# Pairs of heads in one two-bank PSUM tile, and the output projection begun with attention and retention instead of pooling and convolution

## The chip, the cores and the metric

The kernel runs on one core of a Trainium2 chip. The metric is device time in microseconds (us) for one launch. Lower is better. The engines are called as the profile calls them: PE is TensorE (PEld its weight loads), DVE is VectorE, ACT is ScalarE, POOL is GpSimd, SP is SyncE, whose queue issues nearly all DMAs here.

## The reference, cut to what matters

Two layers of a decoder trunk, 512 tokens, model width 1024, all in float32. In each layer four mixers of 256 channels read one input projection, and one output projection reads the four of them side by side:

```python
h = rmsnorm(x, norm_mix_g[l]) * (1.0 + sc1) + sh1
u = h @ w_in[l]
fq, fk, fv, ff, pu, rq, rk, rv, rg, cu = jnp.split(u, bounds, axis=-1)
y_fox  = fox_attention(fq, fk, fv, ff, fox_fb[l])       # 4 heads x 64, forgetting attention
y_pool = pool_mixer(pu, pool_w[l], pool_scale[l])       # causal means over 2/4/8/16 tokens
y_ret  = retention(rq, rk, rv, rg, positions, ret_gn_g[l])   # 4 heads x 64, chunks of 128
y_conv = conformer_conv(cu, conv_w[l], ...)             # GLU, depthwise 31 taps, LayerNorm, swish
mix = jnp.concatenate([y_fox, y_pool, y_ret, y_conv], axis=-1)
x = x + g1 * (mix @ w_out[l])
h = rmsnorm(x, norm_ffn_g[l]) * (1.0 + sc2) + sh2
x = x + g2 * ((jax.nn.silu(h @ ffn_w1[l]) * (h @ ffn_w3[l])) @ ffn_w2[l])
```

The shifts, scales and gates (sh, sc, g) are products of the vector c with a 1024 x 6144 matrix in each layer, and a last RMSNorm follows.

## The kernel before

**Layout.** Activations are held transposed: 128 channels on the partitions, 512 tokens along the free axis, eight such chunks. Each large operand is split into a high part that fits the fast fp32r format and a low rest (`yh`, `yl` for the normed input, `ah`, `al` for mixer outputs, `wh`, `wl` for weights), and each product is three matmuls, `mm3`, lines 265 to 267: high x high, low x high, high x low. Weights come through the SP queue into `raw`, ACT casts `wh` (line 164), DVE subtracts `wl` (line 169); `plan` lists them in the order of their use, `take` and `rel` walk along it. The small products of attention and retention are plain float32 matmuls, and each leaves two records in the trace.

**PSUM.** Eight banks: a ring "mm" of three for projection results (`bank`), a ring "sm" of four for everything else (`small`), and one bank `aux` for sums of a few columns.

**Order of the work.** The text emits the projections in the order of the list `MO` (`pu` pooling input, `rk`, `rq`, `rv`, `rg` retention's key, query, value and gate, `o` two columns of the first half of the output projection). Beside them run generators: `conv_gen` (31 taps as DVE steps of two per yield, line 740, then a LayerNorm, lines 744 to 763), `fox_gen` (attention), `ret_gen` (one for each pair of retention's heads), `pool_mix`, and `ada_gen` (modulation sums on DVE, line 320, from `ada` tiles that DMA brings). Each call of `slot()` after a projection or half of one advances every generator by its rate (`r_conv`, `r_fox` and so on for layer 0, `q_...` for layer 1); `finish_bg` runs one to its end. `FB` steps of attention are emitted as soon as it starts. This text order is what the program states as priority: the last lines of the kernel pass `schedule_with_timeline_sim=True`, so a planner may issue ready work of lower priority earlier on an engine, and each engine then runs its list in order.

**Attention.** For each pair of heads and each block i of 128 queries: `scores` multiplies (line 812, one matmul for each head on 64 rows of the array, into a `small` each), reduces and normalises on DVE and ACT (lines 818 to 829); `turn` transposes the probabilities (line 838) and copies them to "PT" (line 840); `weigh` multiplies with the values (line 850, 64 columns for each head) into one bank held over the four blocks, which `split` turns into a pair of `ah` and `al` after the last. The steps of neighbouring blocks overlap.

**Output projection.** Columns of 128 outputs read eight mixer chunks: 0 and 1 attention, 2 and 3 pooling, 4 and 5 retention, 6 and 7 convolution. The first pass (`do_o`) takes pooling and convolution, chunks 2, 3, 6, 7, for all eight columns and adds them to the residual (line 1052); its first call finishes pooling and convolution. The second pass takes chunks 0, 1, 4, 5 with `N1` columns' banks open at first, finishing attention before chunk 0 and retention before chunk 4. Then follow the second norm and the feed-forward part in three segments; `adaV` generators (rate `r_adaV`, `q_adaV`) sum the remaining modulations beside it, and the end of the first segment finishes whatever runs.

Of the kernel before, what the change touches and what calls it, by code (L numbers as in the profile page):

```python
# [33 lines left out]
KN = {'GA': 3, 'GA1': 3, 'TR': 'V', 'NH': 5, 'NH1': 5, 'ST': ((0, 1), (1, 1), (2, 2), (4, 1), (5, 1), (6, 1), (7, 1)), 'MO': 'pu rk rq rg rv o o o o', 'MO1': 'pu rk rv rq o o o rg o', 'GK': 4, 'RD': 'sync', 'MM': 3, 'SM': 4, 'FB': 1, 'FB1': 2, 'OUTP': 0.0, 'FRONT': 1, 'FRONT1': 0, 'r_rot': 2, 'r_ada': 0.6, 'r_conv': 0.7, 'r_fox': 0.85, 'r_ret': 1, 'r_pool': 0.3, 'r_adaV': 0.4, 'q_conv': 1, 'q_fox': 1.2, 'q_ret': 2, 'q_pool': 0.4, 'q_adaV': 1, 'bP': 4, 'bPT': 2, 'bt': 3, 'brx': 2, 'bmx': 6, 'br8': 4, 'bpl': 3, 'brP': 3, 'bada': 3, 'bacs': 3, 'NR': 2, 'NW': 4, 'N1': 3, 'N11': 1, 'YLG': 9, 'SC': ('AVPPPGPA', 'GGPAVVPP', 'VVVVVVPP', 'VVVVVGVP', 'AAVPAVVP', 'VVVVVVVP', 'VVVVVVVP', 'AAVPAVVP'), 'SH': ('AVAPPPPP', 'VPPPPPAP', 'AAGAAAPP', 'AAAAAAPP', 'AAAAAAGP', 'AVVGAAVG', 'AAAAAAPP', 'AAAAAAPP'), 'MS': '', 'OF': {'lc': -1.907, 'lwq': -2.817, 'lw': -2.364, 'lh': -2.036, 'sc': -1.65, 'ds': 0.034, 'sh': -2.846, 'pc': -0.763, 'mc': -2.466, 'ph': -0.991, 'mh': 0.907, 't': 0.871, 'yh': -1.858, 'yl': 0.927, 'wh': -0.208, 'wl': -2.386, 'whq': -1.469, 'wlq': -0.219, 'mm': 0.333, 'mq': -0.566, 'dq': 0.84}, 'KB': (-4.084, -0.552, 1.672, 3.163, 4.202, 4.915, 6.134, 7.492), 'OA': (1, 0, 2, 3), 'OA1': (0, 1, 3, 2), 'OB': (1, 2, 0, 3), 'OB1': (1, 3, 0, 2), 'OUTP1': 3.0}  # L34
# [3 lines left out]
BUFS = dict(pw=2, ada=KN["bada"], ared=2, qk=4, acs=KN["bacs"], v=2, ff1=1, ff2=1, ff3=1, ff4=1, cumD=2, P=KN["bP"], rP=KN["brP"], PT=KN["bPT"], mx=KN["bmx"], cb=1,  # L38
# [7 lines left out]
def trunk(ctx, tc, x, c, positions, ada_w, ada_b, norm_mix_g, norm_ffn_g, w_in, fox_fb,  # L46
# [26 lines left out]
    def bank():  # L73
        return ps.tile([P, S], F32, tag="mm", name=nm("mm"), bufs=KN["MM"])
# [4 lines left out]
    def banks_of(n):  # L79
        return [bank() if i < KN["MM"] else small() for i in range(n)]  # L80
# [105 lines left out]
    for l in range(DEPTH):  # L186
        lstart.append(len(plan))
        if l == 0:
            for kh in range(2):
                plan += [wcol(w_in, 0, COL["cu"], 512, kh * 4 + k, 1) for k in range(4)]  # L190
                plan.append(wcol(w_in, 0, COL["fq"], 256, kh * 4, 4))
        else:
            plan += [wcol(w_in, l, n0) for n0 in CU]
            plan += [wcol(w_in, l, j * P) for j in range(2)]
        plan += [wcol(w_in, l, COL["fk"] + j * P) for j in range(2)]
        plan += [wcol(w_in, l, COL["fv"], 260, 4 * kh, 4) for kh in range(2)]
        outs = 0
# [8 lines left out]
        plan += [wout(l, i, 0) for i in range(4)]  # L206
# [25 lines left out]
    cur = dict(layer=0, on=0.0)  # L232
# [548 lines left out]
    def fox_gen(l, q, k, v):  # L781
# [17 lines left out]
        cds, prob, prT, outp = {}, {}, {}, {}  # L799
# [6 lines left out]
        def scores(pair, i):  # L806

            w = (i + 1) * P
            sts = [small(), small()]
            for hh in range(2):  # L810
                r0 = 64 * hh
                PE.matmul(sts[hh][:, 0:w], q[pair][r0:r0 + 64, i * P:w], k[pair][r0:r0 + 64, 0:w], start=True, stop=True)  # L812
            for hh in range(2):
                h, st = 2 * pair + hh, sts[hh]
# [17 lines left out]
        def turn(pair, i):  # L832
            w = (i + 1) * P
            for h in (2 * pair, 2 * pair + 1):
                pr = prob.pop((h, i))
# [3 lines left out]
                prT[h, i] = tmp("PT")  # L839
                A.copy(prT[h, i][:, 0:w], tt[:, 0:w])  # L840

        def weigh(pair, i):

            if i == 0:
                outp[pair] = small()
            pts = [prT.pop((2 * pair + hh, i)) for hh in range(2)]
            for j in range(i + 1):
                for hh in range(2):
                    h = 2 * pair + hh
                    PE.matmul(outp[pair][64 * hh:64 * hh + 64, i * P:(i + 1) * P], v[:, j, h * 64:(h + 1) * 64],  # L850
                              pts[hh][:, j * P:(j + 1) * P], start=j == 0, stop=j == i)
            if i == 3:
                mix[pair] = act_pair(pair)
                split(mix[pair], outp[pair])
# [34 lines left out]
    def ret_gen(l, pair, q, k, vbox, outs, sg):  # L889
# [11 lines left out]
        sts = [small(), small()]  # L901
        for n in range(4):
            for hh in range(2):
                r0 = 64 * hh
                PE.matmul(sts[hh][:, n * P:(n + 1) * P], k[r0:r0 + 64, n * P:(n + 1) * P],
                          q[r0:r0 + 64, n * P:(n + 1) * P], start=True, stop=True)
        prs = []
        for hh in range(2):
            h = 2 * pair + hh
            pr = tmp("rP")  # L910
            V.tensor_tensor(out=tri(pr, P), in0=tri(sts[hh], P),
                            in1=tri(cs[:, C_DM + h * P:C_DM + (h + 1) * P], P).to_broadcast([P, 4, P]), op=ALU.mult)
            prs.append(pr)
# [22 lines left out]
        for n in range(4):  # L936
            for hh in range(2):
                h = 2 * pair + hh
                PE.matmul(po[64 * hh:64 * hh + 64, n * P:(n + 1) * P], v[:, n, h * 64:(h + 1) * 64],
                          prs[hh][:, n * P:(n + 1) * P], start=n == 0, stop=False)  # L940
# [122 lines left out]
    for l in range(DEPTH):  # L1063
        cur["layer"] = l
        cur["on"] = 0.0
        early = []
# [79 lines left out]
        def do_o():  # L1146
            if not outs:
                finish_bg(pg)
                finish_bg([cg])
# [71 lines left out]

        start_bg("adaV", ada_gen(l, (5,)))
# [105 lines left out]
```

## Time and profile before

| | |
|---|---|
| median of 3 runs | 1254.05 us (1253.93 to 1257.28) |
| the profiled execution | 1255.27 us, of which the span is 1253.5 us |
| PE busy | 1209.0 us, 96% |
| DVE busy | 761.2 us, 61% |
| ACT busy | 406.5 us, 32% |
| mean granted PE clock | 0.974 |

The page cuts the span into 40 equal slices and gives the busy share of each engine in tenths; PEclk is the clock that PE was granted, in tenths of full speed. The views of the trace list instructions as line, engine, operation, and output <- inputs by the program's tile names; x2 after a row is a count, and brackets hold idle time before the row and what ended it. Lines are those of the kernel before.

### The profile page before, as it was taken

What the parts mean: (1) busy time and instruction counts of PE and PEld (TensorE: products, weight loads), DVE (VectorE), ACT (ScalarE), POOL (GpSimd) and SP (SyncE); (2) the same over time, 40 slices, a digit from 0 to 9 for tenths busy, and PEclk for the clock granted to TensorE, in tenths of its full rate; (3) what the DMA queues carried; (4) which work ended last, traced back from release to release, by engine and by line L of the source; (5) the groups of instructions that cost most, each with busy time, mean ns of one, the idle gap of its engine ahead of it and who ended that gap; (6) DMA issues with size and microseconds to landing.
All of it is one profiled execution on the core that took longest, in us unless ns stands there. A gap on an engine that the chain in (4) does not pass through costs nothing.

```text
span 1253.5 us, 16762 instructions
## 1 busy us (share of the span) xinstructions
PE 1209.0 (96%) x6373; PEld 1004.1 (80%) x6373; DVE 761.2 (61%) x1332; ACT 406.5 (32%) x654; POOL 95.5 (8%) x186
## 2 busy tenths in 40 slices
PE   9999989999998999999999999899999999999997
PEld 8778666789876888888899886678988888888887
DVE  6799997577777555453357998457653333333333
ACT  5433334244322222123234244424432223213222
POOL 5432210102000000000000000000100000000000
PEclk8999978999998999999999999899999999999999
DMA  9766622226777545343233343022443323233321
GB/s 308 215 207 187 201 86 76 68 68 190 244 226 239 167 135 173 103 137 97 75 96 95 96 130 84 9 94 84 154 149 101 99 86 99 74 113 101 95 74 68
DMA packets 223721, 160.05 MB, mean 128 GB/s; under 512 B 8374, under 2 KB 198032, under 8 KB 223640
## 3 DMA queue, kind: packets, MB, share of 16 engines
q1 hardware_dynamic: 223464, 158.90, 42.7%
q8 instruction: 50, 0.82, 0.3%
q14 instruction: 31, 0.25, 0.1%
q10 hardware_dynamic: 176, 0.08, 0.0%
HBM read 154.74 MB, written 2.11 MB: 125 GB/s over the span
## 4 chain that ended last, share of the span: by engine, by line
PE 74%; DMA 5%; DVE 4%; issue 1%; ACT 1%; POOL 0%; DVEq 0%; ACTq 0%
PE mm L265 22%; PE mm L266 22%; PE mm L267 22%; DMA ada<-in_ada_w 4%; DVE acs L320 1%; PE sm L812 1%; PE sm L850 1%; PE sm L265 1%; PE sm L266 1%; PE sm L267 1%; DVE wl L169 1%; DMA raw<-in_ffn_w 1%; PE sm L838 1%; PE aux L404 0%; PE sm L961 0%
## 5 line engine op out<-in xcount | busy, mean ns | idle before, releaser
L164 ACT CAST wh<-raw 128x1024 fp32r<-128x1024 f32 (+3 forms) x196 | 198.8, 1015 | 592.4 <-PE mm L266 385.0
L266 PE MATMUL mm<-yl,wh 128*128 128x512 f32 (+1 forms) x984 | 373.1, 381 | 2.2 <-DVE yl L442 2.1
L265 PE MATMUL mm<-yh,wh 128*128 128x512 f32 (+1 forms) x984 | 369.5, 382 | 5.2 <-ACT yh L438 5.2
L267 PE MATMUL mm<-yh,wl 128*128 128x512 f32 (+1 forms) x984 | 372.1, 379 | 0.0
L169 DVE TENSOR_TENSOR wl<-raw,wh 128x1024 fp32r<-128x1024 f32 (+3 forms) x196 | 231.7, 1183 | 137.8 <-ACT wh L164 131.2
L266 PEld LDWEIGHTS mm<-yl,wh 128*128 128x128 f32 x984 | 188.1, 191 | 38.6 <-DVE yl L442 3.5
L265 PEld LDWEIGHTS mm<-yh,wh 128*128 128x128 f32 x984 | 185.4, 191 | 40.6 <-ACT yh L438 6.2
L267 PEld LDWEIGHTS mm<-yh,wl 128*128 128x128 f32 x984 | 188.0, 191 | 36.3 <-issue 0.2
L265 PE MATMUL mm<-ah,wh 128*128 128x512 f32 (+1 forms) x516 | 189.4, 370 | 6.2 <-ACT ah L479 6.2
L266 PE MATMUL mm<-al,wh 128*128 128x512 f32 (+1 forms) x516 | 189.8, 368 | 0.8 <-DVE al L480 0.8
L267 PE MATMUL mm<-ah,wl 128*128 128x512 f32 (+1 forms) x516 | 188.7, 367 | 0.0
L320 DVE SCALAR_TENSOR_TENSOR acs<-ada,cact,acs 128x512 f32<-128x512 f32 x140 | 104.8, 748 | 42.6 <-DMA ada<-in_ada_w 40.4
L1052 DVE SCALAR_TENSOR_TENSOR xT<-mm,mod,xT 128x512 f32<-128x512 f32 (+1 forms) x86 | 57.7, 675 | 117.1 <-PE mm L267 116.8
L265 PEld LDWEIGHTS mm<-ah,wh 128*128 128x128 f32 x516 | 97.3, 189 | 24.0 <-ACT ah L479 6.8
L266 PEld LDWEIGHTS mm<-al,wh 128*128 128x128 f32 x516 | 97.6, 189 | 17.7 <-DVE al L480 1.2
L267 PEld LDWEIGHTS mm<-ah,wl 128*128 128x128 f32 x516 | 97.6, 189 | 17.1 <-issue 0.2
L1232 DVE TENSOR_TENSOR t<-t,mm 128x512 f32<-128x512 f32 x42 | 28.8, 685 | 100.5 <-PE mm L267 100.5
L740 DVE SCALAR_TENSOR_TENSOR hc<-hp,cwT,hc 128x512 f32<-128x512 f32 x120 | 85.3, 745 | 1.0 <-ACT hc L737 0.9
L408 POOL TENSOR_TENSOR r<-r,mhalf 128x2 f32<-128x2 f32 (+3 forms) x16 | 18.1, 1133 | 535.3 <-DVE r L416 535.3
L659 POOL COPY ada<-yl 128x1 f32<-128x1 f32 x80 | 42.0, 531 | 153.7 <-DVE acs L320 103.1
L265 PE MATMUL mm<-wh,yh 128*128 128x256 f32 (+1 forms) x128 | 39.4, 308 | 2.7 <-DVE v L1124 2.7
L438 ACT ACTIVATE yh<-t,mod 128x256 fp32r<-128x256 f32 (+1 forms) x56 | 27.9, 533 | 35.6 <-DVE t L429 27.7
(257 smaller groups left out, 1176.2 us busy)
## 6 DMA issues: line engine op xcount, KB each, us to landing
raw<-in_ffn_w SPq DMA_DIRECT2D x104, 512.0 KB, 4.2
ada<-in_ada_w SPq DMA_DIRECT2D x160, 256.0 KB, 3.4
raw<-in_w_in SPq DMA_DIRECT2D x32, 512.0 KB, 4.2
raw<-in_ffn_w SPq DMA_DIRECT2D x32, 448.0 KB, 3.6
ad<-in_ada_w SPq DMA_DIRECT2D x32, 256.0 KB, 5.9
raw<-in_w_out SPq DMA_DIRECT2D x32, 256.0 KB, 3.1
raw<-in_w_in SPq DMA_DIRECT2D x4, 520.0 KB, 4.4
xn<-in_x SPq DMA_DIRECT2D x4, 512.0 KB, 6.4
```

The source lines that it names most:

```text
L164: A.copy(h[:, 0:n], raw)
L169: V.tensor_tensor(out=lo[:, 0:n], in0=raw, in1=f(h[:, 0:n]), op=ALU.subtract)
L265: PE.matmul(o, lh, rh, start=start, stop=False)
L266: PE.matmul(o, lh, rl, start=False, stop=False)
L267: PE.matmul(o, ll, rh, start=False, stop=stop)
L320: V.scalar_tensor_tensor(out=acc, in0=r, scalar=ck, in1=acc, op0=ALU.mult, op1=ALU.add)
L408: G.tensor_tensor(out=out_, in0=ms, in1=mhalf[:, 0:ms.shape[-1]], op=ALU.pow)
L438: A.activation(yh[k][:, u:v], y, AF.Identity, bias=shift(l, i, k), scale=1.0)
L659: G.tensor_copy(t_[:, 0:1], f(yl[k][:, at:at + 1]))
L740: V.scalar_tensor_tensor(out=hcs[j], in0=hps[j][:, t:t + S], scalar=cwT[:, l, j, t:t + 1], in1=hcs[j], op0=ALU.mult, op1=ALU.add)
L1052: V.scalar_tensor_tensor(out=xT[:, n, u:v], in0=b[:, u:v], scalar=mod[l][:, gcol + n:gcol + n + 1], in1=xT[:, n, u:v], op0=ALU.mult, op1=A ...
L1232: V.tensor_tensor(out=t_, in0=t_, in1=b3, op=ALU.mult)
```

## The change

- The first pass of the output projection takes chunks 0, 1, 4, 5 (attention, retention) and its first call finishes those generators; the second takes 2, 3, 6, 7 (pooling, convolution), finishing pooling before chunk 2 and convolution before chunk 6. The weights' plan follows. `MO` is `rk rq rv rg pu o o o o` in both layers, and the orders `OA`, `OB` of the four chunks are new.
- PSUM: "mm" has two banks, "sm" three, and a new tile "pp" of two neighbouring banks holds the scores of a pair of heads, in attention and in retention; it also lends its banks to groups of four projections. In the feed-forward part (`wide`) every third `bank()` comes from "sm".
- Attention's transposed probabilities of a pair share one tile. The first head's products also wait, by an added dependency, for the second head's copy. `weigh` uses a bank for each block and splits each block by itself. Retention's mask is one DVE instruction for a pair.
- Rates: in layer 0 `r_ada` 0.6 to 0.45, `r_conv` 0.7 to 0.65, `r_fox` 0.85 to 1.2, `r_adaV` 0.4 to 0.7, `FB` 1 to 2; in layer 1 `q_conv` 1 to 0.65. From the first output product on, convolution and modulation advance by 2.0 for each slot (`LATE`).
- The ring "rP" shrinks from three to two, with "rQ" new.

The values in the long dictionary `KN` that differ, and the code:

```diff
-'MO': 'pu rk rq rg rv o o o o', 'MO1': 'pu rk rv rq o o o rg o', 'MM': 3, 'SM': 4, 'FB': 1,
-'r_ada': 0.6, 'r_conv': 0.7, 'r_fox': 0.85, 'r_adaV': 0.4, 'q_conv': 1,
-'OA': (1, 0, 2, 3), 'OA1': (0, 1, 3, 2), 'OB': (1, 2, 0, 3), 'OB1': (1, 3, 0, 2)
+'MO': 'rk rq rv rg pu o o o o', 'MO1': 'rk rq rv rg pu o o o o', 'MM': 2, 'SM': 3, 'FB': 2,
+'r_ada': 0.45, 'r_conv': 0.65, 'r_fox': 1.2, 'r_adaV': 0.7, 'q_conv': 0.65,
+'OA': (0, 2, 1, 3), 'OA1': (0, 2, 1, 3), 'OB': (0, 1, 2, 3), 'OB1': (0, 1, 2, 3)
+LATE = dict(conv=2.0, ada=2.0)
...
+    def both():
+        return ps.tile([P, 2, S], F32, tag="pp", name=nm("pp"), bufs=1)
...
+    def bank():
+        turns[0] += 1
+        return small() if cur["wide"] and turns[0] % 3 == 0 else big_bank()
-    def banks_of(n):
-        return [bank() if i < KN["MM"] else small() for i in range(n)]
+    def banks_of(n, wide=True):
+        bs = [big_bank() for _ in range(min(n, 2))]
+        if wide and n > 2:
+            b = both()
+            bs += [b[:, 0], b[:, 1]]
+        return bs[:n] + [small() for _ in range(n - len(bs))]
...
-            e[1] += RATE[cur["layer"]][e[0]] * w * cur["on"]
+            r = LATE.get(e[0]) if cur["part"] else None
+            e[1] += (r or RATE[cur["layer"]][e[0]]) * w * cur["on"]
...
-            sts = [small(), small()]
+            sts = both()
...
         def turn(pair, i):
+            pts = tri(tmp("PT"), S)
...
-                prT[h, i] = tmp("PT")
-                A.copy(prT[h, i][:, 0:w], tt[:, 0:w])
+                cp_ = A.copy(pts[:, hh, 0:w], tt[:, 0:w])
+            prT[pair, i] = pts, cp_
...
-                outp[pair] = small()
+                mix[pair] = act_pair(pair)
+            po = small()[:, 0:P]
...
-                    PE.matmul(outp[pair][64 * hh:64 * hh + 64, i * P:(i + 1) * P], v[:, j, h * 64:(h + 1) * 64],
-                              pts[hh][:, j * P:(j + 1) * P], start=j == 0, stop=j == i)
-            if i == 3:
-                mix[pair] = act_pair(pair)
-                split(mix[pair], outp[pair])
+                    m = PE.matmul(po[64 * hh:64 * hh + 64, :], v[:, j, h * 64:(h + 1) * 64],
+                                  pts[:, hh, j * P:(j + 1) * P], start=j == 0, stop=j == i)
+                    if hh == 0:
+                        tc.add_manual_dep(m.ins, cp_.ins.name, SYNC, reason="both heads at once")
+            split([p_[:, i * P:(i + 1) * P] for p_ in mix[pair]], po)
...
         def do_o():
             if not outs:
-                finish_bg(pg)
-                finish_bg([cg])
+                finish_bg(rgens)
+                finish_bg([fg])
+                cur["part"] = 1
...
-                    prod_out(b, h, lo, c, q, (2, 3, 6, 7)[q], 0, S, q == qs[0], q == qs[-1])
+                    prod_out(b, h, lo, c, q, (0, 1, 4, 5)[q], 0, S, q == qs[0], q == qs[-1])
...
-        banks = banks_of(N1)
+        banks = banks_of(N1, False)
...
             if q == 0:
-                finish_bg([fg])
+                finish_bg(pg)
             if q == 2:
-                finish_bg(rgens)
+                finish_bg([cg])
...
+        cur["wide"] = True
         start_bg("adaV", ada_gen(l, (5,)))
```

More of the change, by code (lines that the diff above doesn't have):

```diff
@@ L37 @@
 RATE = tuple({k[2:]: v for k, v in KN.items() if k.startswith(p)} for p in ("r_", "q_"))
-BUFS = dict(pw=2, ada=KN["bada"], ared=2, qk=4, acs=KN["bacs"], v=2, ff1=1, ff2=1, ff3=1, ff4=1, cumD=2, P=KN["bP"], rP=KN["brP"], PT=KN["bPT"], mx=KN["bmx"], cb=1,
+LATE = dict(conv=2.0, ada=2.0)
+BUFS = dict(pw=2, ada=KN["bada"], ared=2, qk=4, acs=KN["bacs"], v=2, ff1=1, ff2=1, ff3=1, ff4=1, cumD=2, P=KN["bP"], rP=2, rQ=1, PT=KN["bPT"], mx=KN["bmx"], cb=1,
             vs=1, t=KN["bt"], pl=KN["bpl"], rx=KN["brx"], hp=2, hc=2, st=2, r8=KN["br8"])
@@ L71, in tmp, with big_bank @@
         return t_[:, 0:full if w is None else w]
-    def bank():
+    cur = dict(layer=0, on=0.0, part=0, wide=False)
+    turns = [0]
+    def both():
+        return ps.tile([P, 2, S], F32, tag="pp", name=nm("pp"), bufs=1)
+    def big_bank():
         return ps.tile([P, S], F32, tag="mm", name=nm("mm"), bufs=KN["MM"])
@@ L205, in trunk @@
                 plan += [wcol(w_in, l, COL[n] + j * P) for j in range(2)]
-        plan += [wout(l, i, 0) for i in range(4)]
+        plan += [wout(l, i, 1) for i in range(4)]
         f0 = 0
@@ L808, in scores @@
             w = (i + 1) * P
-            sts = [small(), small()]
+            sts = both()
             for hh in range(2):
                 r0 = 64 * hh
-                PE.matmul(sts[hh][:, 0:w], q[pair][r0:r0 + 64, i * P:w], k[pair][r0:r0 + 64, 0:w], start=True, stop=True)
+                PE.matmul(sts[:, hh, 0:w], q[pair][r0:r0 + 64, i * P:w], k[pair][r0:r0 + 64, 0:w], start=True, stop=True)
             for hh in range(2):
-                h, st = 2 * pair + hh, sts[hh]
+                h, st = 2 * pair + hh, sts[:, hh]
                 cb, cd = cbs[h], cds[h]
@@ L833, in turn @@
             w = (i + 1) * P
-            for h in (2 * pair, 2 * pair + 1):
-                pr = prob.pop((h, i))
+            pts = tri(tmp("PT"), S)
+            for hh in range(2):
+                pr = prob.pop((2 * pair + hh, i))
                 tt = small()
@@ L838, in turn @@
                     PE.transpose(tt[:, j * P:(j + 1) * P], pr[:, j * P:(j + 1) * P], ident)
-                prT[h, i] = tmp("PT")
-                A.copy(prT[h, i][:, 0:w], tt[:, 0:w])
+                cp_ = A.copy(pts[:, hh, 0:w], tt[:, 0:w])
+            prT[pair, i] = pts, cp_
         def weigh(pair, i):
             if i == 0:
-                outp[pair] = small()
-            pts = [prT.pop((2 * pair + hh, i)) for hh in range(2)]
+                mix[pair] = act_pair(pair)
+            po = small()[:, 0:P]
+            pts, cp_ = prT.pop((pair, i))
             for j in range(i + 1):
@@ L900, in ret_gen @@
                          AF.Identity, scale=ccol(4 + 2 * pair + hh))
-        sts = [small(), small()]
+        sts = both()
         for n in range(4):
@@ L904, in ret_gen @@
                 r0 = 64 * hh
-                PE.matmul(sts[hh][:, n * P:(n + 1) * P], k[r0:r0 + 64, n * P:(n + 1) * P],
+                PE.matmul(sts[:, hh, n * P:(n + 1) * P], k[r0:r0 + 64, n * P:(n + 1) * P],
                           q[r0:r0 + 64, n * P:(n + 1) * P], start=True, stop=True)
[L907 to L913, printed above, removed]
+        prs = tri(tmp("rQ"), S)
+        dm = cs[:, C_DM + 2 * pair * P:C_DM + (2 * pair + 2) * P].rearrange("p (h o m) -> p h o m", h=2, o=1)
+        V.tensor_tensor(out=prs.rearrange("p h (n m) -> p h n m", m=P), in0=sts.rearrange("p h (n m) -> p h n m", m=P),
+                        in1=dm.to_broadcast([P, 2, 4, P]), op=ALU.mult)
         yield
@@ L939, in ret_gen @@
                 PE.matmul(po[64 * hh:64 * hh + 64, n * P:(n + 1) * P], v[:, n, h * 64:(h + 1) * 64],
-                          prs[hh][:, n * P:(n + 1) * P], start=n == 0, stop=False)
+                          prs[:, hh, n * P:(n + 1) * P], start=n == 0, stop=False)
         for n in range(1, 4):
@@ L1064, in trunk @@
         cur["layer"] = l
+        cur["part"] = 0
         cur["on"] = 0.0
+        cur["wide"] = False
         early = []
```

16 lines of the change are left out of this document (8 added, 8 removed).

## The prediction

> **What bounds the kernel now.** I read the page's busy shares and slices first, then the windows, then who waited for whom, then the PE timeline inside the two mixing stretches.
>
> ```profile
> span 1253.5 us, 16762 instructions
> ...
> PE 1209.0 (96%) x6373; PEld 1004.1 (80%) x6373; DVE 761.2 (61%) x1332; ACT 406.5 (32%) x654; POOL 95.5 (8%) x186
> ...
> PE   9999989999998999999999999899999999999997
> ...
> DVE  6799997577777555453357998457653333333333
> ...
> PEclk8999978999998999999999999899999999999999
> ```
>
> TensorE works 96% of the span, so the time is nearly the sum of its work; what can be won is its idle 44.5 us, the slices in which its clock is below full, and work of its own that could run side by side. The profiled execution took 1255.27 us, 1.8 us round its span and 1.2 us above the median of 1254.05. I sum against 1255.3.
>
> ```profile
> 150.00:175.00 25.00, 19.13 (x100) 13.83 (x99) 24.97 (x65) 6.14 (x18) 3.91 (x10) 0.83 0.38 114
> 175.00:200.00 25.00, 22.92 (x136) 16.70 (x135) 22.17 (x68) 11.26 (x29) 1.47 (x3) 0.89 0.25 78
> 200.00:225.00 25.00, 21.60 (x158) 16.70 (x156) 17.67 (x40) 10.33 (x20) 4.10 (x8) 0.86 0.17 54
> ...
> 300.00:400.00 100.00, 94.20 (x416) 76.70 (x415) 76.94 (x106) 25.38 (x31) 4.40 (x7) 0.97 0.76 240
> ...
> 775.00:800.00 25.00, 23.06 (x175) 15.20 (x173) 15.53 (x58) 11.99 (x31) 0.00 (x0) 1.00 0.06 21
> 800.00:825.00 25.00, 22.42 (x144) 18.08 (x144) 12.31 (x21) 7.59 (x12) 3.02 (x2) 0.86 0.15 43
> ```
>
> The first columns are the stretch, its length and PE's busy time; the column before the DMA share is the granted clock. The mixers of layer 0 end in 150 to 225, those of layer 1 in 775 to 825. Layer 0: idle 5.87 + 2.08 + 3.40 = 11.35 us, and the clock costs 0.17 x 19.13 + 0.11 x 22.92 + 0.14 x 21.60 = 8.8 us of the busy time. Waste 20.2 us. Layer 1: idle 1.94 + 2.58 = 4.5 us, clock 0.14 x 22.42 = 3.1 us. Waste 7.6 us. In 150 to 175 VectorE is busy 24.97 of 25 us: PE starves because VectorE has too much to do before it. From 200 on VectorE has room. A third idle piece, 5.8 us, lies in 300 to 400.
>
> ```profile
> PE mm L265 <- ACT ah L479: 6.2, 2, 5.8
> ...
> PE mm L265 <- DVE v L1124: 2.7, 1, 2.7
> ```
> ```profile
> 202.00 1.98 PE L746 MATMUL sm<-hc,ones 128*128 128x512 f32 x4
> ...
> 219.86 0.50 PE L266 MATMUL mm<-al,wh 128*128 128x512 f32 x1 [0.76 <-DVE al L480]
> ```
> ```profile
> 796.02 1.98 PE L746 MATMUL sm<-hc,ones 128*128 128x512 f32 x4
> ...
> 812.21 0.96 PE L265 MATMUL mm<-ah,wh 128*128 128x512 f32 x3 [0.39 <-ACT ah L479]
> ```
>
> Layer 0, then layer 1: the convolution's LayerNorm begins on PE at 202.00 and 796.02, and output products go on at 219.86 and 812.21, released by the convolution's splits. For those 16 to 18 us PE has only narrow matmuls. Pooling's products began earlier (190.84, 768.26, the rows of the next fences) and then stood in their banks, half summed. So the convolution, last of the four mixers, gates the first half of the output projection, and the second (attention, retention) waits behind.
>
> **The change, part by part.**
>
> (1) Which half comes first. The output projection is 8 columns x 12 matmuls for each half, 192 in a layer.
>
> ```profile
> 190.84 0.39 PE L265 MATMUL mm<-ah,wh 128*128 128x512 f32 x1
> 191.07 0.39 PE L266 MATMUL mm<-al,wh 128*128 128x512 f32 x1
> ```
> ```profile
> 768.26 0.40 PE L265 MATMUL mm<-ah,wh 128*128 128x512 f32 x1
> 768.50 0.40 PE L266 MATMUL mm<-al,wh 128*128 128x512 f32 x1
> ```
>
> These are output products (they read ah, al); one starts 0.23 us after another, so a half is 96 x 0.23 = 22 us. Before, this work cannot hide the convolution's tail, because it needs it. Afterwards the attention/retention half can. The question is when attention and retention are ready (call it T), and whether the convolution's tail is longer than the cover.
>
> ```profile
> L740 DVE SCALAR_TENSOR_TENSOR hc<-hp,cwT,hc 128x512 f32<-128x512 f32 x56 | 40.9, 744 | 0.0
> L320 DVE SCALAR_TENSOR_TENSOR acs<-ada,cact,acs 128x512 f32<-128x512 f32 x27 | 20.1, 744 | 0.4 <-DMA ada<-in_ada_w 0.3
> L169 DVE TENSOR_TENSOR wl<-raw,wh 128x1024 fp32r<-128x1024 f32 x13 | 15.8, 1219 | 0.8 <-ACT wh L164 0.8
> ```
> ```profile
> L320 DVE SCALAR_TENSOR_TENSOR acs<-ada,cact,acs 128x512 f32<-128x512 f32 x7 | 5.3, 750 | 1.1 <-POOL ada L659 0.6 <-DMA ada<-in_ada_w 0.3
> L829 DVE TENSOR_SCALAR P<-P,mx 128x384 f32<-128x384 f32 (+1 forms) x4 | 1.8, 454 | 0.1
> ...
> L957 DVE SCALAR_TENSOR_TENSOR qk<-sm,vecH,hp 128x512 f32<-128x512 f32 x1 | 0.7, 745 | 0.0
> ...
> L963 DVE TENSOR_TENSOR qk<-qk,sm 128x512 f32<-128x512 f32 x1 | 0.7, 689 | 1.6 <-PE sm L961 1.6
> ```
>
> Layer 0, VectorE. From 87 to 197 it did 56 of the 60 convolution taps and 27 + 3 modulation sums (three first ones stand on a line of their own). By the program's text 30 calls of slot() lie between the convolution's start and the first output product. At the new rate 0.65 they bring 39 taps, where before all 60 were forced ahead of it; at 0.45 they bring 18 of the 48 sums, where 40 were done by 197. That frees (21 + 22) x 0.744 = 32 us. Added ahead of T: the rest of the softmax (four rescalings at 0.45, their reductions: 5 us), the rest of retention (ten 512-wide steps at 0.69 to 0.75: 7 us), eight quarter splits for two whole ones (1 us). 197 - 32 + 13 = 178.
>
> Layer 0, PE: by 198 it had done 18 output matmuls (4 us), carried some 14 us of waste and lacked 12 us of attention and retention: 198 - 4 - 14 + 12 = 192. PE decides. Retention's chain (products, square, sums, root, spread, split, each a hop between engines) ends it, so I take T = 198: 6 us of waste stay. From 178 to 198 VectorE takes taps and sums ahead of their turn (before, 40 sums were done where the rate brought 24), one for one: 13 of the 21 taps left. After T come 8 taps (6 us), as many sums (6 us), weights and residual steps (4 us), the 16 us chain: T + 32. The cover is 22 us and the pooling part of three columns (18 matmuls, 4 us): T + 26, so 6 us idle. 20 - 6 - 6 = 8 us come back. Bounds: all 20; or, with nothing pulled ahead, taps 16, sums 10, other steps 10, chain 16 = T + 52, idle 26: with the 6 us ahead of T, 12 us lost.
>
> Layer 1 has no modulation sums there.
>
> ```profile
> L740 DVE SCALAR_TENSOR_TENSOR hc<-hp,cwT,hc 128x512 f32<-128x512 f32 x60 | 41.5, 746 | 1.0 <-ACT hc L737 0.9
> ```
>
> At 784 PE lacks 17 us of attention and retention and two gate projections (48 matmuls, 11 us), and is 16 output matmuls (4 us) ahead: T = 808. At rate 0.65 and 34 slots 16 taps (12 us) are left, and VectorE, 15.53 of 25 us busy in 775 to 800, can do them by then. The chain ends by T + 16, under a cover of 22. I give back 5 of 7.6 us. Bounds: 7.6; or 12 us of taps and 10 of other steps after T, so T + 38 against 23, 15 idle: 7 us lost.
>
> (2) Pairs in one tile of two banks, and the added wait on the second head's copy.
>
> ```profile
> 188.60 1.09 PE L850 MATMUL sm<-PT,v 128*64 128x128 f32 x14
> ...
> 193.72 0.43 PE L850 MATMUL sm<-PT,v 128*64 128x128 f32 x2
> 194.08 0.91 PE L812 MATMUL sm<-al,al 64*128 64x384 f32 x2
> 194.92 0.43 PE L850 MATMUL sm<-PT,v 128*64 128x128 f32 x2
> 195.29 0.91 PE L812 MATMUL sm<-al,al 64*128 64x384 f32 x2
> ```
> ```profile
> 758.59 0.92 PE L812 MATMUL sm<-ah,ah 64*128 64x384 f32 x4
> ...
> 765.24 1.13 PE L812 MATMUL sm<-ah,ah 64*128 64x512 f32 x4
> ```
> ```profile
> 163.42 1.12 PE L812 MATMUL sm<-ah,ah 64*128 64x512 f32 x2
> ...
> 164.83 1.12 PE L812 MATMUL sm<-ah,ah 64*128 64x512 f32 x2
> ```
>
> Each matmul leaves two records (x2). Both heads issued together take 0.92 us at width 384 (758.59, x4) and 1.13 us at 512; one alone takes 0.91 and 1.12. They run beside each other only when adjacent, and another matmul had slipped between them in eight of the sixteen steps: from start to next start, 0.63 + 1.05 + 0.41 + 0.84 in layer 0 and 0.62 (twice) + 0.41 + 0.84 in layer 1, 5.4 us. The weighting has 16 lone matmuls at 0.36 us; a lone one and an x14 cost 0.36 + 1.02, sixteen together 1.13, so 0.25 us each, 4 us. Ends 0 (PE would have waited there anyway) and 9.4; I take 5, nearer the middle, since the layer 1 half lies where PE is full. The wait puts head 0's products behind head 1's copy; queued behind it on PE is whatever comes next, but without it the pair's second matmul waits at the same place: nothing. With one score tile, the next scores wait for both heads' reductions, 1 to 2 us; projections hide it.
>
> (3) Two banks of projection results instead of three while the mixers run. A projection column is 24 x 0.23 = 5.5 us, and its copy on ScalarE has that long. The retention values take half that and are emptied by VectorE: PE waited 2.7 us there already with three banks. Price 2.5 us (one more such wait), ends 0 and 2 layers x 8 us, if each of four tiles waits the 2 us that a VectorE queue of three steps takes. In the feed-forward part every third column goes to another ring, so a bank is reused after three columns as before: nothing.
>
> (4) Modulation of the next gate at 0.7 a slot instead of 0.4. The 5.8 us wait of PE at 380 ended the sums that were forced out at the end of the first segment:
>
> ```profile
> ACT ah L479 <- DVE t L1232: 20.7, 7, 4.7
> DVE acs L320 <- DMA ada<-in_ada_w: 18.4, 18, 2.8
> ```
>
> With 18 slots, 7 of its 11 steps had their turn before, now all. I take 2 us (the loads may only stand elsewhere in the queue), ends -2 and 5.8 + 3 of half clock behind it.
>
> (5) Smaller: retention's mask once 1024 wide, not twice 512: no fewer elements, nothing. The third ring slot of "rP" at the start falls away; PE has the same first weights to wait for: nothing. Splits in quarters cost VectorE and ScalarE about 1 us a layer, hidden in layer 1, 0.5 us taken.
>
> Sum: 8 + 5 + 5 - 2.5 + 2 - 0.5 = 17 us. 1255.3 - 17 = 1238.
>
> **A rule against it.** In 150 to 225 the clock is 0.83 to 0.89, yet the longest single wait of PE there is the 2.7 us of L1124. The clock may be low because the matmuls there are narrow and not because PE waits; then the narrow ones, which the change keeps, keep it low. The clock's share of the waste is (8.8 + 3.1) / 27.8 = 43%, and of the 13 us given back 5.6 would stay: 1244. The Trainium skill, "TensorE: Matmul & The Clock Gate", section "Why this matters for your kernels", says that gaps of more than about 3 us drop the clock; by it none of these gaps would have, which speaks for this case. The trace shows drops without such a gap.
>
> **Rivals.**
> - The waits only move: VectorE's total in the stretch is unchanged, and PE waits after the first half for what it waited for ahead of it. Then (1) gives nothing and the rest 4 us: 1251. For it: 24.97 of 25 us in 150 to 175. Against: VectorE's 17.67 of 25 after 200, room that is now unused.
> - Slower, the convolution's tail: with its taps and the sums both at 2.0 a slot, one output column (2.8 us of PE) puts four taps and up to three sums on VectorE, 5 us. If it reaches T with no tap taken ahead, the second half waits 26 us in layer 0 and 15 in layer 1: 12 + 7 us lost, 4 won by the rest, 1270; halfway between no change and that, 1262. It turns the sum once layer 0's taps end more than 33 us after T (10 are covered; 14, 5 and 4 are what layer 0, layer 1 and the rest bring). Against it: 24.97 of 25 us in 150 to 175, VectorE does not idle while taps are ready.
> - Two banks: 16 us of waits by (3) in place of 2.5: 1252.
>
> **How the numbers follow.** Forecast, 1230 to 1247: 0.52. Clock stays low, 1244: 0.10. Waits only move, 1251: 0.17, half of it within 0.3%, which is about what a measurement can tell here (1250.3 to 1257.8). Two banks, 1252: 0.05, mostly the same. Slower tail, 1262 and more: 0.16. Faster 0.71, same 0.12, slower 0.17. For 8 in 10 the range leaves out most of the slow tail and a little of full return at the low end (20 + 7.6 + 9.4 back would be near 1220): 1222 to 1260.
>
> **What would show it.** Right: an output product that reads attention and retention starts near 198 and 808; PE's idle in the two mixing stretches falls under 10 us together and the clock row there is over 0.95; score matmuls stand as x4 at 0.92 and 1.13; the 5.8 us wait on ah is gone. Wrong: PE waits on the convolution's split between the halves for more than 10 us, on VectorE for a projection bank, or the first output product starts later than 205.

## The result: 1276 us, slower by 1.6%, and the profile after

The changed kernel takes 1276.3 us (median), the kernel before on the same chip 1255.7; the ratio is 1.016 (1.012 to 1.019). I had forecast 1238. The times below are medians without slow runs; only e11 had one, of 2523.7 us, and its 1268.2 in the expectation of e16 is the median with that run in. The profiled execution took 1277.9 us, its span is 1276.1. The head of its page:

```profile
span 1276.1 us, 16746 instructions
...
PE 1204.1 (94%) x6373; PEld 1001.0 (78%) x6373; DVE 762.3 (60%) x1340; ACT 408.6 (32%) x666; POOL 91.4 (7%) x186
...
PE   8989678989997999999999999988999999999997
...
DVE  6889885667777765433356987556763333342333
...
PEclk7989889799998999999999999999999999999999
```

PE's busy time fell by 4.9 us (1209.0 to 1204.1), yet the span rose by 22.6: idle time went from 44.5 to 72.0 us. Where, shows in the windows (length, PE busy, PEld, DVE, ACT, POOL, then granted clock, DMA share, GB/s):

```profile
125.00:150.00 25.00, 14.52 (x90) 12.24 (x89) 21.11 (x49) 3.43 (x7) 3.56 (x6) 0.86 0.56 165
150.00:175.00 25.00, 21.41 (x124) 16.26 (x123) 24.80 (x62) 10.67 (x26) 0.27 (x3) 0.93 0.23 74
175.00:200.00 25.00, 21.70 (x142) 14.93 (x140) 18.57 (x74) 11.32 (x32) 0.11 (x1) 0.93 0.13 43
200.00:225.00 25.00, 20.77 (x196) 17.07 (x197) 13.24 (x25) 6.43 (x13) 6.12 (x13) 0.96 0.33 106
225.00:250.00 25.00, 23.33 (x79) 16.78 (x76) 17.52 (x28) 7.01 (x10) 1.96 (x11) 0.70 0.30 97
...
825.00:850.00 25.00, 20.95 (x112) 15.19 (x109) 13.47 (x24) 5.74 (x9) 2.08 (x5) 0.93 0.13 42
```

The same two stretches in the kernel before:

```profile
125.00:150.00 25.00, 25.00 (x122) 18.89 (x122) 24.26 (x51) 9.22 (x15) 6.81 (x12) 1.00 0.68 212
225.00:250.00 25.00, 25.00 (x161) 19.34 (x160) 13.58 (x20) 5.05 (x7) 1.76 (x2) 1.00 0.27 85
```

A new hole stands in 125 to 150 (10.5 us idle, before none), and 225 to 250, full before at clock 1.00, has clock 0.70. The list of what PE waited for, over the whole span, has at its top:

```profile
PE mm L284 <- DVE v L1144: 7.9, 3, 3.6
PE sm L284 <- ACT ah L498: 6.2, 1, 6.2
...
PE mm L284 <- ACT rx L1132: 4.8, 2, 4.1
...
PE pp L831 <- DVE mx L841: 2.8, 1, 2.8
```

The columns are the sum, the number and the longest. The longest waits on `v`, `rx` and `mx` (3.6, 4.1 and 2.8 us) fill the hole in 125 to 150; before there was one on `v`, of 2.7. The wait on `ah` is the one near 380 that my prediction let go: 6.2 us, before 5.8. PE's timeline at the end of layer 0's mixers (start, us, line):

```profile
202.05 1.09 PE L957 MATMUL sm<-rQ,v 128*64 128x128 f32 x16
...
205.41 0.39 PE L284 MATMUL mm<-ah,wh 128*128 128x512 f32 x1
...
209.90 1.04 PE L979 MATMUL sm<-ident,r 128*64 128x128 f32 x16
210.87 0.66 PE L917 MATMUL sm<-ident,qk 128*128 128x128 f32 x4
...
219.83 0.44 PE L962 MATMUL sm<-qk,st 64*64 64x128 f32 x4 [1.00 <-DVE st L948]
220.96 1.05 PE L969 MATMUL aux<-hones,t 128*128 128x2 f32 x8 [0.69 <-ACT t L965]
...
224.00 1.98 PE L979 MATMUL sm<-ident,r 128*64 128x128 f32 x16 [0.27 <-POOL r L427]
...
229.33 1.20 PE L284 MATMUL mm<-ah,wh 128*128 128x512 f32 x2
...
233.91 0.80 PE L284 MATMUL mm<-ah,wh 128*128 128x512 f32 x1 [1.67 <-DVE xT L1070]
```

Line 957 is retention's masked scores times values, 969 its sums of squares, 979 the spreading of the roots, its last step on PE. Retention's first pair of heads ends with the row at 209.90. The second starts, with its transposes, at 210.87 (line 917), ends with the row at 224.00, and only at 229.33 do whole columns of the output projection run. The products between 205 and 218 are those of attention and the first pair, whose banks then stand half summed. Layer 1 has the same picture:

```profile
821.29 1.09 PE L979 MATMUL sm<-ident,r 128*64 128x128 f32 x16
822.31 0.66 PE L917 MATMUL sm<-ident,qk 128*128 128x128 f32 x4
...
830.35 1.05 PE L969 MATMUL aux<-hones,t 128*128 128x2 f32 x8 [0.70 <-ACT t L965]
833.38 1.68 PE L979 MATMUL sm<-ident,r 128*64 128x128 f32 x16 [1.97 <-POOL r L427]
...
836.49 1.13 PE L284 MATMUL mm<-ah,wh 128*128 128x512 f32 x2
```

To compare kernels I cut each span at the first GLU of the convolution and the first SiLU of the feed-forward part of each layer (length in us, in brackets PE's idle time). The first cut slides with the order of the projections; where it does, add the first two columns.

| profiled execution | start | mixing 0 | feed-forward 0 | mixing 1 | rest |
|---|---|---|---|---|---|
| before | 74.1 (7.5) | 222.0 (14.4) | 383.1 (6.9) | 215.6 (7.1) | 358.8 (8.5) |
| after | 77.3 (11.3) | 232.0 (27.0) | 388.4 (11.7) | 217.7 (12.9) | 360.8 (9.2) |
| e1 pairs only | 76.3 (10.1) | 229.7 (23.6) | 388.0 (13.4) | 223.5 (15.2) | 360.8 (8.7) |
| e2 order only | 73.8 (9.0) | 233.2 (18.7) | 385.3 (11.3) | 219.5 (11.0) | 357.8 (7.5) |
| e7 two banks | 77.2 (7.0) | 226.3 (16.8) | 397.8 (16.7) | 224.4 (11.9) | 362.1 (8.0) |
| e8 swap | 74.1 (7.4) | 230.5 (19.2) | 384.2 (11.8) | 218.8 (7.8) | 358.0 (7.7) |
| e9 after, freed | 77.3 (9.4) | 220.8 (21.9) | 389.2 (13.1) | 207.3 (9.3) | 360.7 (8.9) |
| e10 flat, 2 + 5 | 75.5 (6.3) | 233.8 (33.5) | 384.6 (10.6) | 221.9 (14.7) | 360.1 (8.1) |
| e14 swap, freed | 72.5 (5.0) | 232.7 (23.9) | 384.1 (10.4) | 214.2 (5.5) | 358.6 (7.6) |
| e15 order, freed | 73.5 (5.3) | 226.7 (21.6) | 383.9 (10.5) | 208.3 (5.5) | 358.5 (8.2) |
| e16 flat, 3 + 4, freed | 81.6 (6.6) | 211.6 (18.4) | 386.2 (10.3) | 210.2 (10.4) | 360.2 (8.2) |

### The profile page after: what moved, and what is told of

The parts are those of the page before. It is cut to its first block, busy times and chain, and to the rows that moved or that the text cites. A ratio compares the mean times of both kernels' runs of the same rounds, so it can differ in the third digit from the quotient of the medians.

```text
span 1276.1 us, 16746 instructions
## 1 busy us (share of the span) xinstructions
PE 1204.1 (94%) x6373; PEld 1001.0 (78%) x6373; DVE 762.3 (60%) x1340; ACT 408.6 (32%) x666; POOL 91.4 (7%) x186
## 4 chain that ended last, share of the span: by engine, by line
PE 65%; DMA 4%; DVE 2%; issue 1%; ACT 1%; POOL 0%; DVEq 0%; SPq 0%; ACTq 0%
PE mm L284 15%; PE mm L285 14%; PE mm L286 14%; PE sm L284 5%; PE sm L285 5%; PE sm L286 5%; DMA ada<-in_ada_w 3%; PE pp L284 1%; PE pp L286 1%; PE pp L285 1%; DVE acs L339 1%; PE pp L831 0%; PE sm L871 0%; DVE wl L188 0%; PE sm L858 0%
## 5 line engine op out<-in xcount | busy, mean ns | idle before, releaser
L284 PE MATMUL mm<-yh,wh 128*128 128x512 f32 (+1 forms) x704 | 268.0, 386 | 8.9 <-ACT yh L457 6.1
L285 PE MATMUL mm<-yl,wh 128*128 128x512 f32 (+1 forms) x704 | 269.1, 384 | 3.0 <-DVE yl L461 2.9
L286 PE MATMUL mm<-yh,wl 128*128 128x512 f32 (+1 forms) x704 | 268.2, 382 | 0.0
L284 PEld LDWEIGHTS mm<-yh,wh 128*128 128x128 f32 x704 | 134.0, 193 | 34.4 <-ACT yh L457 6.7
L285 PEld LDWEIGHTS mm<-yl,wh 128*128 128x128 f32 x704 | 135.2, 193 | 31.0 <-DVE yl L461 4.8
L286 PEld LDWEIGHTS mm<-yh,wl 128*128 128x128 f32 x704 | 135.1, 192 | 27.5 <-issue 1.8
L285 PE MATMUL mm<-al,wh 128*128 128x512 f32 (+1 forms) x378 | 142.3, 376 | 1.4 <-DVE al L499 1.4
L284 PE MATMUL sm<-yh,wh 128*128 128x512 f32 x240 | 94.6, 395 | 0.0
L286 PE MATMUL sm<-yh,wl 128*128 128x512 f32 x240 | 94.1, 392 | 0.0
L285 PE MATMUL sm<-yl,wh 128*128 128x512 f32 x240 | 94.0, 392 | 0.0
L1254 DVE TENSOR_TENSOR t<-t,mm 128x512 f32<-128x512 f32 x28 | 19.2, 685 | 62.9 <-PE mm L286 62.9
L286 PEld LDWEIGHTS sm<-yh,wl 128*128 128x128 f32 x240 | 45.1, 188 | 10.3
```

Source lines behind the costliest of these rows:

```text
L284: PE.matmul(o, lh, rh, start=start, stop=False)
L285: PE.matmul(o, lh, rl, start=False, stop=False)
L286: PE.matmul(o, ll, rh, start=False, stop=stop)
L1254: V.tensor_tensor(out=t_, in0=t_, in1=b3, op=ALU.mult)
```

## The experiments

The letters in the expectations: A, later T, is that the swapped output projection starts with work that is ready too late; B that the projections miss their third bank; C that the place of the pooling projection in `MO` did it; P that the single two-bank tile holds up the scores; S that the order of before is a fine balance which any edit upsets; M that each loss has a place of its own; D that VectorE is full, so that nothing can be won by starting earlier.

**Each half of the change alone.** e1 is the changed kernel with the order, `MO` and rates of before, e2 the kernel before with the new order, `MO`, rates and `LATE`:

```diff
 # e1, in the changed kernel
-'MO': 'rk rq rv rg pu o o o o', 'MO1': 'rk rq rv rg pu o o o o'
+'MO': 'pu rk rq rg rv o o o o', 'MO1': 'pu rk rv rq o o o rg o'
...
-                finish_bg(rgens)
-                finish_bg([fg])
+                finish_bg(pg)
+                finish_bg([cg])
...
-                    prod_out(b, h, lo, c, q, (0, 1, 4, 5)[q], 0, S, q == qs[0], q == qs[-1])
+                    prod_out(b, h, lo, c, q, (2, 3, 6, 7)[q], 0, S, q == qs[0], q == qs[-1])
 # e2, in the kernel before: these edits the other way round
```

> The kernel after with its tiles (pairs in one two-bank tile, two projection banks, three small ones, the wait for both copies, quarter splits) but with the order of the mixers, the order of the output projection and all rates of before. Theory A (the order loses: the first half of the output projection now waits for retention, whose second pair is the last link, and nothing is left to cover it): the pairs gain what side-by-side matmuls give, so 1247 to 1256 us. Theory B (two projection banks lose: projections wait until a bank is emptied): 1264 us or more, with over 8 us more idle on PE before the first output product than before.

1279.2 us, ratio 1.016 (1.014 to 1.019): the time that B had forecast.

> The kernel before with the order of the mixers, of the output projection and the rates of after, but its old tiles: three projection banks, four small ones, each head by itself. Theory A: 1268 to 1284 us, and the first full column of the first half comes after 220 us in layer 0, released by retention's second pair. Theory B: 1248 to 1258 us.

1272.9 us, 1.011 (1.008 to 1.015): the time that A had forecast, and whole output columns run from 225.4 on. So either half alone loses nearly as much as both; the losses don't add. Each has its own cause, or the order of before can't be touched at all.

**Two quick guesses that fell.** e3 is the changed kernel with `pu` first in both lists, e4 with `'MM': 3, 'SM': 2`.

> The kernel after with pooling's projections moved back to the head of the mixers (layer 0 pu rk rq rg rv, layer 1 pu rk rq rv rg). Theory C (the rotations of retention's keys now come first, and PE stands while their DMAs and the bank copies behind them are late: 10.5 us idle in 125 to 150): that idle falls under 4 us and the time by 6 to 10 us, to about 1268. Theory A: retention ends later still, so 1276 to 1285.

1279.7 us, 1.018 (1.015 to 1.021): C falls.

> The kernel after with three projection banks and two small ones instead of two and three. Theory B: 10 us or more come back (1266 or less). Theory A: between 1271 and 1283, as the waits for retention stay.

1278.7 us, 1.015 (1.012 to 1.019), inside A's range. A third projection bank taken from the small ones wins nothing; with the two-bank tile apart, five others are all there is to divide.

**A repeat, and one suspect at a time, in the kernel before.** e5 was meant as a control.

```diff
-'r_conv': 0.7, 'q_conv': 1        # e5
+'r_conv': 0.69, 'q_conv': 0.98
-'FB': 1, 'r_ada': 0.6, 'r_conv': 0.7, 'r_fox': 0.85, 'r_adaV': 0.4, 'q_conv': 1      # e6
+'FB': 2, 'r_ada': 0.45, 'r_conv': 0.65, 'r_fox': 1.2, 'r_adaV': 0.7, 'q_conv': 0.65
-'MM': 3, 'SM': 4                  # e7
+'MM': 2, 'SM': 5
 # e8: the change's edits of plan, do_o, OA, OB, LATE; MO1 'pu rk rv rq rg o o o o'; nothing else
```

> The kernel before with two rates moved by 2% (r_conv 0.7 to 0.69, q_conv 1 to 0.98) and nothing else: the same work, the same tiles, but about 1850 of PE's and 632 of DVE's places in the order move. A control. Theory S (the order of before is a fine balance and nearly any other order of the same work loses): 1264 us or more. Theory M (each loss has a place and a cause of its own, and an order near the old one costs what the old one did): 1252 to 1261.

1257.4 us, 1.000 (0.998 to 1.001). But the edit did nothing: in the traces of the kernel before and of e5, every engine runs the same operations of the same lines in the same order (6373 records on PE, 1332 on DVE, no place differs). The 1850 places of the expectation aren't there. So e5 is a second sample of the kernel before, and S stays open until e13, where the order does change.

> The kernel before with only the changed kernel's rates and FB (r_ada 0.45, r_conv 0.65, r_fox 1.2, r_adaV 0.7, q_conv 0.65, FB 2). Theory S: 1265 to 1275, like every change so far. Theory M with the rates as the cause of the order kernel's +15: 1268 or more; with the swap as its cause: 1253 to 1262, and the stall on ah near 380 gone, which my prediction had laid to r_adaV (1249 to 1255 if only that acts).

1265.9 us, 1.006 (1.004 to 1.008), in S's range and between those of M: the rates cost some 8 us in the order of before, half of e2's loss. The stall on `ah` near 380 is not gone.

> The kernel before with two projection banks and five small ones, nothing else. Theory B (the third projection bank is what the pairs cost): 1265 to 1278, with waits of PE for DVE at projections. Rival P (the single two-bank tile, which chains scores to the max of the block before, is the cost): 1252 to 1262. Theory S: 1264 or more.

1289.0 us, 1.024 (1.021 to 1.028), more than I had given B. Nearly half of it lies in layer 0's feed-forward part (383.1 to 397.8), where this kernel has no third bank to borrow:

```profile
PE sm L838 <- DVE P L829: 8.1, 9, 2.2
PE mm L265 <- DVE t L1232: 6.7, 5, 2.1
...
PE mm L265 <- ACT rx L1112: 5.1, 3, 2.1
```

Line 265 begins a projection, and `t`, `rx` are what DVE and ACT were doing when PE wanted the bank; before, the first and the third of these rows stood at 2.6 us and not at all.

> The kernel before with the halves of the output projection swapped (attention and retention first, new orders of chunks, convolution and modulation at 2.0 after the first product), with its own tiles, rates and layer 0's list; layer 1's list ends in rg o o o o. Theory T (attention and retention end after PE has run out of other work, so the swap opens a hole before the first output product): 1266 to 1276, the mixing of layer 0 longer by 8 us or more, that of layer 1 by 3 or more. Rival (the rates and the moved pooling projection did that, the swap itself is worth what I predicted): 1240 to 1256.

1270.4 us, 1.010 (1.008 to 1.013): T's numbers, in layer 0 (8.5 us) and layer 1 (3.2). What is ready too late differs: in layer 1 it is retention's second pair, whose last step on PE begins at 837.85; in layer 0 that pair is at 223.55, and the last products of attention begin at 232.29, right before whole columns at 234.28.

**The cause taken away.** In the changed kernel `ret_gen` holds the second pair back until the first is done. e9 lets it go:

```diff
-        while (pair == 1 and 0 not in outs) or len(k) <= pair or len(q) <= pair:
+        while len(k) <= pair or len(q) <= pair:
...
-        prs = tri(tmp("rQ"), S)
+        prs = tri(tmp("rQ"), S) if pair == 0 else None    # pair 1: held("ah7"), held("al7"), two masks
```

> The changed kernel, but retention's second pair of heads no longer waits for the first to be finished; its masked scores go to tiles of their own (ah7, al7, written by the convolution later) by two DVE instructions. Theory T (the hole before the output products is retention's second pair, serial behind the first): its records end 5 us or more earlier, the mixing of layer 0 shortens from 232.0 by 4 to 9 us, 1265 to 1272. Rival D (DVE is full in 150 to 200, so what starts earlier only pushes something else later): within 4 us of the changed kernel, 1272 to 1280.

1258.6 us, 1.001 (0.999 to 1.003): 18 us of the 21 are gone, more than I had expected of T. The timeline of e9, layer 0 and layer 1 (lines 975 and 985 are 969 and 979 of the changed kernel):

```profile
207.33 1.02 PE L975 MATMUL aux<-hones,t 128*128 128x2 f32 x8
...
210.29 1.09 PE L985 MATMUL sm<-ident,r 128*64 128x128 f32 x16
...
212.30 1.09 PE L985 MATMUL sm<-ident,r 128*64 128x128 f32 x16
...
213.88 1.02 PE L284 MATMUL mm<-ah,wh 128*128 128x512 f32 x2
```
```profile
813.73 1.09 PE L985 MATMUL sm<-ident,r 128*64 128x128 f32 x16
...
815.52 1.04 PE L985 MATMUL sm<-ident,r 128*64 128x128 f32 x16
...
817.06 1.03 PE L284 MATMUL mm<-ah,wh 128*128 128x512 f32 x2
```

The two pairs now end 2 us apart, and whole columns run at 213.88 and 817.06, 15.5 and 19.4 us earlier. Of the 20.7 us between the two spans (1276.1 and 1255.4) PE's idle time gives 9.4 and its busy time 11.3 (1204.1 to 1192.8): the granted clock is up from 0.966 to 0.973 on average.

**The banks, in the changed kernel.** e10 gives the tile of two banks back to the small ring (2 + 5, the two heads' scores in two `small()`), e11 is the same with 3 + 4; e12 drops the added wait.

```diff
-            sts = both()            # e10 and e11, in scores and ret_gen
+            sts = [small(), small()]
-'MM': 2, 'SM': 3
+'MM': 2, 'SM': 5                   # e11: 'MM': 3, 'SM': 4
-                    if hh == 0:     # e12
-                        tc.add_manual_dep(m.ins, cp_.ins.name, SYNC, reason="both heads at once")
```

> The changed kernel with the two-bank tile given back to the ring of small banks: two projection banks, five small ones, the scores of the two heads in two banks of that ring. Rival P (the single two-bank tile, which lets no second block of scores start before the first is read, is what the pairs cost): 1264 to 1271. Theory B (a bank fewer for projections is the cost, wherever the others go): 1274 to 1292.

1277.5 us, 1.016 (1.014 to 1.018), in B's range: P falls as the whole cost.

> As the kernel with two projection and five small banks, but three and four, the division of the kernel before; every third bank of the feed-forward part still comes from the small ones, and probabilities of a pair still share a tile. Theory B: 1266 to 1274, like the kernel that had the new order alone. If the pairs' shared probabilities and the added wait cost, not the banks: 1275 or more.

1267.4 us, 1.008 (1.006 to 1.009): B. The third projection bank is worth 10 us here.

> The changed kernel without the added wait of the first head's products for the second head's copy. My prediction costed the wait at nothing: 1272 to 1280. If it holds up attention's chain (28 products of 128 columns behind 8 copies a layer), 1264 to 1271.

1282.6 us, 1.020 (1.018 to 1.021), above both ranges: nothing to win there; why it comes out above the changed kernel was not tried.

**What is left of the swap without the serial pairs.** e13 is the kernel before, e14 is e8, e15 is e2, e16 is e11, each with the second pair freed (e13 to e15 with `'brP': 6` for the masked scores, e16 as in e9).

> The kernel before with retention's second pair no longer waiting for the first, and six tiles rP in place of three. Theory T (the serial pairs cost only where the output projection begins with retention): 1250 to 1260. If it is a cost of its own, swap or not: 1236 to 1247.

1259.6 us, 1.001 (1.000 to 1.002). The second pair's transposes start at 178.54 in place of 223.17, and retention's last step at 236.30 in place of 248.55 (layer 1: 824.55 in place of 843.27), and the time stays. So in the order of before the serial pairs cost nothing, as T says. This is also the control that e5 was not: about 1180 of PE's 6373 records stand in another place than in the kernel before, and S, which forecast 1264 or more, falls.

> The kernel with the swapped halves alone (1270.4), with retention's second pair freed. Theory T with the swap worth what I predicted: 1240 to 1250. T with the swap worth nothing by itself: 1253 to 1260. If the swap's loss there is something else (convolution's tail, modulation): 1265 or more.

1264.5 us, 1.005 (1.003 to 1.007): 6 us better than e8, but not the 20 that I had predicted, and just short of the third case, that something else makes most of this kernel's loss. The gain is all in layer 1's mixing (218.8 to 214.2 us); start and mixing 0 together are 305.2 us, in e8 304.6. The trace of e14 shows why:

```profile
223.46 1.09 PE L963 MATMUL sm<-ident,r 128*64 128x128 f32 x16
...
231.82 1.11 PE L852 MATMUL sm<-PT,v 128*64 128x128 f32 x16
234.47 0.96 PE L267 MATMUL mm<-ah,wh 128*128 128x512 f32 x3 [1.53 <-ACT ah L481]
```

Line 963 is retention's last step, 852 attention's products with the values. At the old rates attention ends last in layer 0, with or without the second pair freed.

> The kernel with the new order and rates and the old tiles (1272.9), with retention's second pair freed. By T 10 to 18 us less: 1254 to 1262; 3 to 10 us above the swap alone with the pair freed, if the rates cost their 8 us there too.

1256.6 us, 0.999 (0.997 to 1.000): 16 us better than e2. Against expectation it lies below e14: the new rates and `MO`, a loss in the old order, are worth 8 us once the second pair is free. In layer 0 the place shows: attention's last products (line 852) start at 209.4, where in e14 they start at 232.7, and whole columns run from 215.94 on, not from 234.47. Whether attention's own rate does this or the lower rates of convolution and modulation, which leave VectorE to it, was not tried.

> The changed kernel with three projection and four small banks, no two-bank tile (1268.2), and retention's second pair freed. If the gains of the two add up (18 and 8): 1249 to 1254, faster than before. If they are the same microseconds: 1256 to 1264.

1252.6 us, 0.995 (0.994 to 0.997): the two gains nearly add up (1276.3 - 18 - 9 = 1249), and this kernel beats the one before by 5 us. What PE waits for in its mixing of layer 0:

```profile
PE sm L870 <- ACT PT L858: 2.7, 4, 1.0
PE sm L916 <- DVE mx L840: 1.8, 1, 1.8
PE sm L857 <- DVE P L847: 1.8, 2, 0.9
...
PE mm L283 <- ACT rx L1135: 1.3, 1, 1.3
```

The wait on `v` is gone and that on `rx` is 1.3 us.

## Why the prediction was wrong, step by step

**The step that failed: T, in part (1).** I took attention and retention as ready at 198 and 808. They were ready at 229 and 836. My ledger added up the PE work that was still to do (12 and 17 us) and, in layer 0, granted 6 us for a chain in which each step is a "hop between engines"; that is one chain for both pairs of heads, and the code runs the pairs one behind the other. One pair takes 18.5 us from its transposes to whole output columns in layer 0 (210.87 to 229.33) and 14.2 in layer 1 (822.31 to 836.49), with 6 to 7 us of its own PE work in it. Two of my signs of being wrong came with it: the first output product of layer 0 starts at 205.41, and PE waits on VectorE for projection banks (`v`). Rows of the kernel before could have told me. Retention's last step on PE (line 961, all of them; duration as min/median/max, then first and last start):

```profile
L961 PE MATMUL sm<-ident,r x64: 272/273/477, 222.1 to 844.1; 128*64 128x128 f32 x64
```
```profile
222.15 1.09 PE L961 MATMUL sm<-ident,r 128*64 128x128 f32 x16
223.17 0.55 PE L896 MATMUL sm<-ident,qk 128*128 128x128 f32 x3
```

It began at 222.1 in layer 0 and went on to 844.1 in layer 1: late already, and free because the half of pooling and convolution came first. The second row is the second pair's first step, its transposes, right behind the first pair's end. e9 (the wait gone: -18 us) and e13 (the wait gone without the swap: nothing) show this cause for the changed kernel. The swap alone has another one beside it in layer 0, attention, which e14 shows. Even freed, T is 214 and 817, so the ledger was short by another 16 and 9 us; that rest I haven't taken apart.

The other end of (1) was right: the convolution's tail is covered. In the changed kernel its LayerNorm started on PE at 245.89 and 849.18 and PE was full from 250 to 275. The rival that ended slower than before, by that tail, has the right sign by the wrong mechanism. With T mended, layer 1 gives back 7.2 us (e15, 215.6 to 208.3), inside my 5 with an upper end of 7.6; in layer 0, start and mixing 0 together are 2.1 us longer than before in e9, 4.2 in e15, and 2.8 shorter in e16 with three banks and shared probabilities, where I had 8 back.

**Part (3), two banks: mis-sized.** I took 2.5 us with an upper end of 16. Alone, they cost 31 (e7); in the changed kernel, giving the third one back is worth 10 (e10 against e11), and with retention freed 6 (e9 against e16). What I missed is how often a bank waits for an engine whose queue is long. The wait on `v`, the one I had singled out, grew from 2.7 to 7.9 us; `rx` and the one score tile added 4.8 and 2.8. The latter I had called hidden. That the feed-forward part loses nothing when every third column borrows a bank was nearly right: e10 with five small banks to borrow from is 1.5 us longer there, e7 without borrowing 14.7; the changed kernel, with three small ones, 5.3. The 3.2 us at the start may be banks, too: e7 has 3.1 of them with all its "rP" slots; but e10, with two projection banks and five small ones, has 1.4, and its order differs from e7's.

**Part (2), the pairs: right, but not thanks to the tile of two banks.** The score matmuls stand together, as I had said they would:

```profile
186.18 0.92 PE L831 MATMUL pp<-al,al 64*128 64x384 f32 x4
...
192.36 1.13 PE L831 MATMUL pp<-al,al 64*128 64x512 f32 x4
```

PE's busy time fell by 4.9 us, near my 5 (though the clock enters that number as well). But e10, whose two heads write two separate banks, has them together, too:

```profile
190.29 0.92 PE L830 MATMUL sm<-al,al 64*128 64x384 f32 x4
...
197.13 1.13 PE L830 MATMUL sm<-al,al 64*128 64x512 f32 x4
```

So the tile of two banks isn't needed for that, and the bank that it took from the projections bought nothing that a run shows. What the new tiles are worth with three projection banks shows in e11 against e2 and in e16 against e15, which have the same order and rates: 5 and 4 us less. That is the size I had taken, though the added wait, the quarter splits and the borrowed banks of the feed-forward part are in that difference as well.

**Part (4), the rate of the next gate's sums: wrong.** The wait on `ah` near 380 is 5.8, 8.3 and 8.7 us at 0.4 (before, e8, e14) and 6.2, 6.7, 7.5 and 7.6 at 0.7 (after, e6, e2, e15). The new rate doesn't shorten it; the one pair that differs in rates alone, before and e6, has 5.8 and 6.7. In the kernel before VectorE stood 13.3 us in 340 to 400 waiting for the `ada` tiles from DMA, at a DMA share of 0.76 over 300 to 400; that the loads set this wait is likely but was not tried.

**The clock.** My rival "clock stays low" had the sign: over the whole span the clock is 0.966, before 0.974. In the changed kernel it is 0.70 in 225 to 250, where PE idles 1.67 us in all, one wait of 1.7. The Trainium skill, "TensorE: Matmul & The Clock Gate", section "Why this matters for your kernels", warns of idle gaps over about 3 us. The trace agrees in 125 to 150, where waits of 3.6 and 4.1 us go with 0.86. It doesn't in 225 to 250, where the deeper drop comes behind narrow matmuls (219.83 to 224.00 above) and waits of 1.7 us or less. That narrow matmuls do it is not shown either. In e9, from 216.14 to 222.47, PE runs wide output products alone, behind waits of 0.5, 0.7 and 1.3 us (before 216.14, 219.94 and 222.47), and still they slow down:

```profile
223.06 0.63 PE L285 MATMUL mm<-al,wh 128*128 128x512 f32 x1
223.49 0.63 PE L286 MATMUL mm<-ah,wl 128*128 128x512 f32 x1
```

One starts 0.43 us after another there, where it was 0.23. What the many short waits and the narrow matmuls each do to the clock stays open.

## What to carry to other kernels

Before moving work A ahead of work B, find in the trace when A's last step ends now, not how much work it has left: a chain of small steps over four engines has a length of its own, and a generator's "wait until the other is done" doubles it without a row in the list of waits as long as something else covers it. A PSUM bank given away for a few microseconds of faster matmuls has to be priced at the longest queue of the engine that empties it. Change the order, the rates and the banks one at a time, too: here the rates lost 8 us in the old order and, with `MO`, won 8 in the new one once the second pair was free. And see in the trace that an edit meant as a control did change something.

## What the runs showed that I had not expected

- With the second pair freed in the kernel before, some 1180 of PE's 6373 records stand in another place, and the time is the same to 0.2% (e13). Two rates moved by 2% moved none (e5).
- Taking waits away can win more than their idle time: of e9's 20.7 us, 11.3 are PE's own busy time, at a granted clock of 0.973 in place of 0.966, with the same number of PE instructions.
